# RWKV layers: loras on scaled weights, products beside the block solution, four recurrence lanes, fewer read-back transfers

## The chip, the core and the metric

The kernel runs on one core of one Trainium2 chip. Five engines work from queues of their own, each in the order of its program: TensorE (matrix products into PSUM), VectorE, ScalarE, GpSimd and SyncE, and 16 DMA engines move data for all of them. An engine that comes to an instruction whose input is not there waits, and all that is queued behind it on that engine waits too. The metric is the device time of one execution in microseconds; the time of before is the median of three runs.

## What is computed

The reference is a block of four layers, each with a feed-forward part, a mixer and a second feed-forward part, and a second block behind them, over 256 tokens of width 1024 in float32. The mixers of layers 0 and 3 are RWKV-7, and the change touches only these:

```python
dx = token_shift(h) - h
xr, xw, xk, xv, xa, xg = [h + dx * mu[j] for j in range(6)]
r, k, v = xr @ w_rkv[0], xk @ w_rkv[1], xv @ w_rkv[2]
w = -jax.nn.softplus(-(w0 + jnp.tanh(xw @ w1) @ w2)) - 0.5
decay = jnp.exp(-jnp.exp(w.astype(f32)))
a = jax.nn.sigmoid(a0 + (xa @ a1) @ a2)
v = v + (v_first - v) * jax.nn.sigmoid(v0 + (xv @ v1) @ v2)   # layer 3 only
g = jax.nn.sigmoid(xg @ g1) @ g2
# 16 heads of 64: a state of 64 x 64 per head, updated token by token from
# decay, k, v, a and the normalised direction of k * k_k, and read by r;
# then a norm over the head, a bonus (r * k * r_k) summed times v, times g, @ w_o
```

## The kernel before

Tensors lie transposed, channels on the partitions: eight tiles of 128 channels by 256 tokens, so tile k holds heads 2k and 2k+1. A projection is done in split precision: weights and inputs are cut into a high and a low part, and each product is three matmuls (`mm3`, L379 to L381). A weight tile `raw` (128x1024) is loaded on SyncE's queue, its high part `wh` made by ScalarE (L292), the low part `wl` by VectorE (L371); three `raw` buffers are in turn. One tile of a projection takes eight such triples, 24 matmuls.

The recurrence is done in chunks of 64 tokens, four per tile. Within a chunk the token-by-token dependence is a triangular system of 64 unknowns per head and chunk, cut into two halves of 32. The program of one RWKV layer, `rwkv(l, j)`, in its order:

- *keys*: `mixed(2)` makes h, dx and the split key input (L670 to L675); `project(1)` follows tile by tile. `plain` (L684) makes the mixed inputs xw and xa of the decay and rate loras, `lora` (L697) and `lora_up` (L707) their two products each. `directions` (L748 to L753) norms the keys. Some steps of the first four value products (`values`, tile name `pval`) are beside them.
- *decay and factors*: a running sum of the log decays (L761, a scan), its exponentials (L763 to L772), and the scaled keys, directions and receptances of each pair of tiles (`factors`, L782 to L785, one of them on GpSimd). A product `pd` (L793) gives the triangular matrices, which ScalarE copies and stores to DRAM as dL (L798).
- *solution*: `solve` loads dL back as LT, one system per partition (L809, ScalarE's queue), and does forward substitution in 31 steps of two VectorE operations (L821, L822), each over all 128 systems. Results T and U are stored to DRAM (dTU, L826) and read back by head (L835 and L836, 24 loads of 32 partitions on ScalarE's queue). Beside it stand the receptance products (`project(0)`; `receive`, L876, multiplies them in), `grams` (L890 on TensorE, masked by VectorE in L891) and the gate's mixed input.
- *lanes*: `recur(k)` for each tile: bonus product `bo` (L922) of `rk` (L918), turning keys and values to token order (`tok` L930, `tokv` L938), `inverse` (px L904, pt L909: the half of the inverse that couples the two halves of 32), then four chunks, each with products `pc` for the right side (L951, L954), the solution (L959), the new state (L964) and the output (L973, L975). Three lanes work side by side, `LANES = ((0, 3, 6), (1, 4, 7), (2, 5))`, starting 0, 4 and 8 steps late; the remaining four values, the closing of each pair of tiles (head norm, bonus, gate product `pgt`) and the output projection `pjrwo` are woven into them.

`weave` calls a list of generators in turn, one step each; this and the builder's own scheduling set the order in which instructions stand on each engine. Names: GM are the masked grams, SR the receptances and scaled directions, AK the scaled keys, UV the values and solved rows by token, `st` the state.

## Time and profile before

| | |
|---|---|
| median of the runs | 3050.86 us (3048.76 to 3070.9) |
| the profiled execution | 3068.02 us, span 3066.2 us |
| mean granted clock of TensorE | 0.963 |
| TensorE / VectorE / ScalarE / GpSimd busy | 2889.8 / 2245.3 / 1587.3 / 64.3 us |
| RWKV of layer 0 | 225 to 538.9 us of the span |
| RWKV of layer 3 | 2045 to 2359.6 us |

A window row gives, for one stretch, the busy time of each engine with the number of instructions, then the granted clock as a share of full speed and the share of the DMA engines. The clock is at one of two levels, 1.2 or 2.4 GHz, so that 0.50 means the lower one throughout. A busy share says nothing of who waits for whom; for that the profile has waits, each with the instruction that ended it.

### The profile page before, as it was taken

Reading aid. Unit: us, or ns where it says so; the run is one execution under the profiler, and the core shown is the slowest. Engines: PE = TensorE matmul, PEld = TensorE weight load, DVE = VectorE, ACT = ScalarE, POOL = GpSimd, SP = SyncE. Lnnn points to the kernel's source line nnn. Section 1 sums busy time; section 2 is a strip of 40 time slices with the busy share of each in tenths; the row PEclk is TensorE's granted clock in tenths of the full one; section 3 lists DMA queues with packets and bytes.
Section 4 is the critical chain, followed back from the end, with each engine's and each line's share of the span. In section 5 each row is a group of like instructions: output and inputs, shape, how many; then the busy total and the mean of one; then the engine's idle time right before and its main releaser. Section 6 shows DMA issues by size and latency. Waiting matters only on the chain. (4 is left out here: it accounts for less than half of the span.)

```text
span 3066.2 us, 57996 instructions
## 1 busy us (share of the span) xinstructions
PE 2889.8 (94%) x23318; PEld 2736.4 (89%) x23318; DVE 2245.3 (73%) x3912; ACT 1587.3 (52%) x2746; POOL 64.3 (2%) x71
## 2 busy tenths in 40 slices
PE   7999699999998999999999999989599999999998
PEld 6987577999997989999988999988488999889898
DVE  8888724888787888888887888787635767566754
ACT  5547134545446765455466545446145546644543
POOL 0000000000000100000000000000000000000000
PEclk9999779999999999999999999999699999999899
DMA  8983312787884547887844887864303665544464
GB/s 320 333 308 106 103 33 75 258 298 265 295 278 158 165 142 223 293 289 278 297 157 143 289 310 256 295 204 126 91 23 121 199 183 179 180 144 130 152 185 132
DMA packets 196031, 614.47 MB, mean 200 GB/s; under 512 B 41137, under 2 KB 45105, under 8 KB 195762
## 3 DMA queue, kind: packets, MB, share of 16 engines
q1 hardware_dynamic: 169234, 596.54, 59.1%
q10 hardware_dynamic: 24544, 7.87, 1.1%
q0 software_dynamic: 1984, 6.36, 0.6%
q8 instruction: 183, 3.00, 0.4%
q14 instruction: 86, 0.70, 0.1%
HBM read 604.36 MB, written 6.32 MB: 199 GB/s over the span
## 5 line engine op out<-in xcount | busy, mean ns | idle before, releaser
L292 ACT ACTIVATE wh<-raw 128x1024 fp32r<-128x1024 f32 (+3 forms) x859 | 887.0, 1036 | 948.5 <-DMA raw<-in_wi 239.9
L371 DVE TENSOR_TENSOR wl<-raw,wh 128x1024 fp32r<-128x1024 f32 (+3 forms) x859 | 1030.5, 1202 | 388.7 <-ACT wh L292 381.6
L380 PE MATMUL pjwi<-xl,wh 128*128 128x256 f32 x2568 | 722.3, 283 | 3.9 <-DVE xl L504 3.5
L381 PE MATMUL pjwi<-xh,wl 128*128 128x256 f32 x2568 | 718.1, 281 | 0.2 <-DVE wl L371 0.2
L379 PE MATMUL pjwi<-xh,wh 128*128 128x256 f32 x2568 | 714.6, 282 | 3.2 <-ACT xh L292 1.8
L380 PEld LDWEIGHTS pjwi<-xl,wh 128*128 128x128 f32 x2568 | 483.7, 189 | 6.4 <-DVE xl L504 6.2
L381 PEld LDWEIGHTS pjwi<-xh,wl 128*128 128x128 f32 x2568 | 484.7, 189 | 0.4 <-DVE wl L371 0.4
L379 PEld LDWEIGHTS pjwi<-xh,wh 128*128 128x128 f32 x2568 | 480.0, 189 | 3.8 <-ACT xh L292 2.0
L380 PE MATMUL pdwo<-gl,wh 128*128 128x256 f32 x1408 | 395.6, 281 | 0.0
L381 PE MATMUL pdwo<-gh,wl 128*128 128x256 f32 x1408 | 395.5, 281 | 0.0
L379 PE MATMUL pdwo<-gh,wh 128*128 128x256 f32 x1408 | 394.7, 280 | 0.0
L420 DVE SCALAR_TENSOR_TENSOR aring<-aring,cbc 128x1024 f32<-128x1024 f32 x286 | 343.4, 1219 | 3.2 <-DMA aring<-in_adaw 3.0
L379 PEld LDWEIGHTS pdwo<-gh,wh 128*128 128x128 f32 x1408 | 265.4, 188 | 0.0
L380 PEld LDWEIGHTS pdwo<-gl,wh 128*128 128x128 f32 x1408 | 265.1, 188 | 0.0
L381 PEld LDWEIGHTS pdwo<-gh,wl 128*128 128x128 f32 x1408 | 264.8, 188 | 0.0
L381 PE MATMUL pjw2i<-xh,wl 128*128 128x256 f32 x416 | 118.8, 286 | 0.0
L379 PE MATMUL pjw2i<-xh,wh 128*128 128x256 f32 x416 | 118.2, 284 | 0.0
L380 PE MATMUL pjw2i<-xl,wh 128*128 128x256 f32 x416 | 117.7, 283 | 0.0
L379 PE MATMUL pjmbi<-xh,wh 128*128 128x256 f32 x352 | 101.1, 291 | 6.2 <-DVE cv L1076 3.7
L380 PE MATMUL pjmbi<-xl,wh 128*128 128x256 f32 x352 | 101.7, 290 | 0.6 <-DVE xl L504 0.6
L381 PE MATMUL pjmbi<-xh,wl 128*128 128x256 f32 x352 | 99.7, 284 | 0.3 <-DVE wl L371 0.3
L292 ACT ACTIVATE gh<-g 128x256 fp32r<-128x256 f32 x198 | 80.1, 405 | 33.5 <-DVE g L596 20.0
(516 smaller groups left out, 5922.2 us busy)
## 6 DMA issues: line engine op xcount, KB each, us to landing
raw<-in_wi SPq DMA_DIRECT2D x352, 512.0 KB, 4.6
aring<-in_adaw SPq DMA_DIRECT2D x286, 512.0 KB, 5.3
raw<-in_wo SPq DMA_DIRECT2D x128, 512.0 KB, 4.8
raw<-in_w2i SPq DMA_DIRECT2D x56, 512.0 KB, 3.8
raw<-in_wo SPq DMA_DIRECT2D x64, 384.0 KB, 4.5
raw<-in_rkv SPq DMA_DIRECT2D x48, 512.0 KB, 4.4
raw<-in_mbi SPq DMA_DIRECT2D x48, 512.0 KB, 3.6
raw<-in_fg SPq DMA_DIRECT2D x22, 512.0 KB, 4.3
```

The source lines that it names most:

```text
L292: ins = self.nc.scalar.activation(out, in_, func, **k)
L371: self.last = self.nc.vector.tensor_tensor(lo, src, hi.bitcast(F32), SUB)
L379: mm(out, a, xh[:parts, k, :], start=start, stop=False)
L380: mm(out, a, xl[:parts, k, :], start=False, stop=False)
L381: mm(out, b, xh[:parts, k, :], start=False, stop=stop)
L420: ins = nc.vector.scalar_tensor_tensor(raw, raw, 1.0, self.cbc, MUL, MUL, accum_out=m[:, b % 24:b % 24 + 1])
```

## The change

1. The first products of the decay and rate loras (w1 and a1) are one matrix `wa1` of 128 columns, and are computed as h times W plus dx times (mu times W): VectorE scales the weights (L694 of the new kernel) in place of mixing the inputs. The gate's input is mixed into dx itself. The second products keep their number.
2. `directions`, `decay` and `factors` follow each other for each pair, two pairs at a time, with 44 of 72 steps of all eight value products beside them.
3. `solve` loads LT in two halves, as soon as each half of the factors is there, in eight loads that alternate between ScalarE's and GpSimd's queues. The stores of T and U go one to each queue. The read-back is six loads of 32 partitions by 32 systems, three on each queue. Beside the steps stand the other values, the first four receptances, the gate's loras, and grams, `bo`, `tok` and `tokv` of the first four tiles (`tokens`).
4. Four lanes work on tiles n and n+4, starting one step apart. The inverse of a tile is a generator of its own ahead of its chunks. Receptances, grams, tokens and inverses of the last four tiles are woven into the lanes. The state is kept by halves of heads: each new state is two operations over 64x64 into a tile that was zeroed once, in place of one of 128x128 by a mask and an addition. The bonus is kept in the values' own tile.

```diff
-LANES = ((0, 3, 6), (1, 4, 7), (2, 5))
-STAGGER = (0, 4, 8)
-FILL = 1
-VALUES = 4
+STAGGER = (0, 1, 2, 3)
+SOLVED = 4
...
+        def lora_wa(dst):
...
+            for k0 in (0, 4):
+                ws.append(self.sp.tile([P, 512], F32, tag="b2", name="wmu", bufs=3))
+                f4 = lambda ap: ap.rearrange("p (k i n) -> p k i n", k=4, i=2)
+                V.tensor_tensor(f4(ws[-1]), f4(w[:, P * k0:P * k0 + 512]), bc(mu[:, k0:k0 + 4, :, None], [P, 4, 2, 64]), MUL)
+            for k in range(KT):
+                mm(ps[:, :T], w[:, k * P:k * P + P], h[:, k, :], start=k == 0, stop=False)
+                mm(ps[:, :T], ws[k // 4][:, k % 4 * P:k % 4 * P + P], dx[:, k, :], start=False, stop=k == KT - 1)
+                yield
...
         def solve():
-            while len(factored) < KT:
-                yield
             LT = self.b8("LT", F32, (P, 2, 1024))
...
-            for c in range(4):
-                self.bounce.dma_start(L[32 * c:32 * c + 32].rearrange("p (i j) -> p i j", j=32),
+            queues = self.bounce, nc.gpsimd
+            for half in range(2):
+                while len(factored) < 4 * half + 4:
+                    yield
+                for c in range(4):
+                    o = 64 * half + 16 * c
+                    queues[c % 2].dma_start(l3[o:o + 16], dL[8 * half:8 * half + 8].rearrange("q (b x) -> (q b) x", b=2)[:, :32 * T].rearrange("g (i x) -> g i x", x=T)[:, :, 64 * c:64 * c + 32])
...
             for u, src in enumerate((Tm, L)):
-                self.bounce.dma_start(dTU[u].rearrange("c g i q -> (c g i) q"), src)
...
-                for c in range(4):
-                    block = lambda u, i: dTU[u, c, o // 8:o // 8 + 8, i].rearrange("g (r t) -> r g t", t=32)
-                    for i in range(2):
-                        self.bounce.dma_start(U[0][o + 32 * i:o + 32 * i + 32, c, :, 32 * i:32 * i + 32], block(1, i))
-                    self.bounce.dma_start(U[1][o:o + 32, c], block(0, 0))
+                queues[u].dma_start(dTU[u].rearrange("h x i q -> (h x i) q"), src)
+
+            for half in range(2):
+                o = 64 * half
+                block = lambda u, i: dTU[u, half, :, i].rearrange("x (r t) -> r x t", t=32)
+                for n, (dst, src) in enumerate(((U[1][o:o + 32], block(0, 0)), (U[0][o + 32:o + 64, :, 32:], block(1, 1)), (U[0][o:o + 32, :, :32], block(1, 0)))):
+                    queues[(n + half) % 2].dma_start(dst, src)
+            solved.append(True)
...
-        weave([keys, chain(plain(1, xw), plain(4, xa), mixed(3, xv)), chain(directions(0), directions(2))])
-        weave([directions(4), directions(6)])
+        weave([keys, chain(*loras), mixed(3, xv)])
...
-        weave([project(0, xr, receive), chain(factors(0), factors(4)), chain(factors(2), factors(6)), solve(), chain(*(grams(k) for k in range(KT))), plain(5, xg)])
+        values_ = chain(*(values(k) for k in range(KT)))
+        ahead = lambda k0: chain(directions(k0), decay(k0), factors(k0))
+        weave([chain(ahead(0), ahead(4)), chain(repeat(None, 2), ahead(2), ahead(6)), islice(values_, 44), chain(repeat(None, 4), mixed(0, xr))])
...
-                    new = q1("st"), None
-                    V.scalar_tensor_tensor(new[0], p4, SC[:, k, c:c + 1], blk, MUL, MUL)
-                    if c:
-                        V.tensor_tensor(new[0], new[0], st[1], ADD)
+                    new = sts[c % 2]
+                    for h_, r in enumerate(H2):
+                        if c:
+                            V.scalar_tensor_tensor(hc(new[r], h_), hc(p4[r], h_), SC[r, k, c:c + 1], hc(old[r], h_), MUL, ADD)
+                        else:
+                            V.tensor_scalar(hc(new[r], h_), hc(p4[r], h_), SC[r, k, c:c + 1], None, MUL)
...
+        rs = project(0, xr, receive, [[i] for i in range(4)])
+        weave([solve(), values_, rs, chain(repeat(None, SOLVED), gates()), chain(*(chain(grams(k), tokens(k)) for k in range(4)))])
...
-        lanes = [chain(repeat(None, n), *(recur(k) for k in lane)) for n, lane in zip(STAGGER, LANES)]
-        weave(lanes + [chain(repeat(None, FILL), *(values(k) for k in range(VALUES, KT)))] + [closing(k) for k in range(0, KT, 2)] + [splits()])
+        lanes = [chain(repeat(None, s), inverse(n), recur(n, sts(n)), recur(n + 4, sts(n))) for n, s in enumerate(STAGGER)]
+        rs = project(0, xr, receive, [[i] for i in range(4, KT)], "ax")
+        weave(lanes + [rs, chain(*(chain(grams(k), tokens(k), inverse(k)) for k in range(4, KT)))] + [closing(k) for k in range(0, KT, 2)] + [splits()])
```

Where instructions come to stand, in the built programs, is shown at three places. First VectorE's row in layer 0 from the end of the factors to the first step of the solution (fs and LT), before:

```order
L813 MEMSET LT 128x1024
L876 TENSOR_TENSOR SR<-SR,pjrkv 128x256
L814 MEMSET LT 128x32
L371 TENSOR_TENSOR wl<-raw,wh 128x1024
L735 TENSOR_SCALAR rest<-par 128x8
L876 TENSOR_TENSOR SR<-SR,pjrkv 128x256
L891 TENSOR_TENSOR GM<-pg,crw 128x512 x14
L876 TENSOR_TENSOR SR<-SR,pjrkv 128x256
L371 TENSOR_TENSOR wl<-raw,wh 32x1024
L821 TENSOR_TENSOR fs<-LT 128x31
```

The same place in the changed kernel, from the last factor (L800):

```order
L800 TENSOR_TENSOR AK<-AK,IP 128x8x64
L752 TENSOR_SCALAR rest<-par 128x8
L906 TENSOR_TENSOR GM<-pg,crw 128x512
L368 TENSOR_TENSOR wl<-raw,wh 128x1024
L906 TENSOR_TENSOR GM<-pg,crw 128x512
L891 TENSOR_TENSOR SR<-SR,pjrkv 128x256
L368 TENSOR_TENSOR wl<-raw,wh 128x1024
L844 TENSOR_TENSOR fs<-LT 128x31
```

Of 14 gram products two are left in front of the first step, and of three receptances one; the others stand among the steps or behind them, the last four tiles' in the lanes.

Second, TensorE's row around the first bonus product `bo`, which waits for VectorE's `rk`; before (ahead of these rows eight triples of `pval`):

```order
L922 MATMUL bo<-rk,cbase 128x256
L930 MATMUL tok<-cbase,AK 128x128 x4
L938 MATMUL tokv<-crw,Vv 64x128 x4
L904 MATMUL px<-T_3844,GM 32x32 x8
L954 MATMUL pc<-UV,GM 64x64
L909 MATMUL pt<-U,X_3967 32x32 x8
```

In the changed kernel (ahead of these rows, since the last `pd`: eight loras, eight gram matmuls and 72 of the split products):

```order
L941 MATMUL bo<-rk,cbase 128x256
L945 MATMUL tok<-cbase,AK 128x128 x4
L712 MATMUL lora<-dx,raw 32x256 x4
L953 MATMUL tokv<-crw,Vv 64x128 x4
L712 MATMUL lora<-dx,raw 32x256 x4
L905 MATMUL pg<-SR,AK 128x128 x8
L941 MATMUL bo<-rk,cbase 128x256
L945 MATMUL tok<-cbase,AK 128x128 x4
L953 MATMUL tokv<-crw,Vv 64x128 x4
L979 MATMUL pc<-UV,GM 64x64 x2
L905 MATMUL pg<-SR,AK 128x128 x8
L941 MATMUL bo<-rk,cbase 128x256
```

Grams and tokens of the first four tiles now stand between the first `bo` and the first inverse. The `rk` of the first `bo` stands on VectorE behind step 22 of 31 (before: in the last step), that of the second in front of the last step, the other two behind the solution.

Third, ScalarE's row around the read-back, before (T and U in all 24 loads, cut here):

```order
L826 DMA dTU_2768<-LT 128x1024 x2
L292 ACTIVATE AK<-tok 128x512
L836 DMA T_3844<-dTU_2768 32x8x32 x2
L835 DMA U<-dTU_2768 32x8x32 x6
L836 DMA T_3844<-dTU_2768 32x8x32
L835 DMA U<-dTU_2768 32x8x32 x2
```

In the changed kernel:

```order
L850 DMA dTU_2764<-LT 128x1024
L289 ACTIVATE AK<-tok 128x512
L289 ACTIVATE UV<-tokv 64x512
L289 ACTIVATE r_3985<-pc 64x128
L856 DMA T_3425<-dTU_2764 32x32x32
L856 DMA U<-dTU_2764 32x32x32 x2
L289 ACTIVATE AK<-tok 128x512
```

Three loads are left on ScalarE, behind three copies that wait for TensorE. The other store and the other three loads stand on GpSimd, behind two zeroings and, of the values, the last store to vf (in layer 3 loads of vf).

## Rows read from the trace of the kernel before

**Rows 1.** Windows, layer 0, one stage each; (x) counts instructions, PEclk the mean clock
```profile
225.00:275.80 50.80, 44.63 (x279) 36.83 (x278) 44.76 (x107) 33.08 (x70) 0.69 (x1) 0.91 0.24 77
275.80:322.70 46.90, 40.95 (x348) 37.40 (x346) 36.96 (x53) 29.85 (x56) 8.46 (x7) 0.93 0.46 148
322.70:344.70 22.00, 21.94 (x189) 20.29 (x191) 13.52 (x25) 1.65 (x2) 0.00 (x0) 0.77 0.23 43
344.70:375.70 31.00, 10.05 (x60) 6.98 (x59) 28.47 (x73) 7.03 (x10) 2.48 (x3) 0.71 0.37 126
375.70:390.20 14.50, 4.18 (x29) 3.15 (x27) 0.82 (x2) 1.27 (x3) 1.80 (x1) 0.62 0.49 118
390.20:538.90 148.70, 146.07 (x1200) 118.05 (x1201) 51.73 (x116) 65.87 (x165) 3.43 (x4) 0.88 0.17 54
```

**Rows 2.** The same windows for the last four stages of layer 3
```profile
2149.30:2170.70 21.40, 21.40 (x179) 19.72 (x175) 12.86 (x23) 1.65 (x2) 0.00 (x0) 0.76 0.23 44
2170.70:2200.90 30.20, 9.05 (x58) 6.22 (x56) 27.52 (x73) 6.77 (x9) 1.89 (x2) 0.71 0.40 123
2200.90:2216.50 15.60, 5.18 (x31) 3.88 (x31) 2.27 (x4) 1.32 (x3) 2.88 (x3) 0.61 0.53 133
2216.50:2359.60 143.10, 141.03 (x1203) 114.98 (x1204) 55.76 (x125) 66.45 (x165) 2.90 (x3) 0.91 0.18 57
```

**Rows 3.** The window in which the lanes of layer 0 begin
```profile
390.00:411.50 21.50, 21.26 (x129) 16.64 (x129) 2.23 (x6) 5.73 (x17) 0.00 (x0) 0.50 0.02 4
```

**Rows 4.** Tile dL, layer 0: ns min/median/max, start times, landing
```profile
L798 ACTq DMA_DIRECT2D dL<-tm x8: 582/618/672, 304.6 to 325.5; - x8
L809 ACTq DMA_DIRECT2D LT<-dL x4: 353/584/709, 328.2 to 329.9; - x4
...
DMA to landing us min/median/max: 2.4/3.6/4.5
```

**Rows 5.** Lines, VectorE, 344.6 to 376: busy us, mean ns, idle before
```profile
L822 DVE TENSOR_TENSOR LT<-LT,fs 128x31 f32<-128x31 f32 (+15 forms) x31 | 10.6, 342 | 0.9
...
L371 DVE TENSOR_TENSOR wl<-raw,wh 128x1024 fp32r<-128x1024 f32 (+1 forms) x5 | 6.1, 1218 | 0.2 <-ACT wh L292 0.2
```

**Rows 6.** A window of projection matmuls alone, columns as in rows 1
```profile
253.00:260.00 7.00, 7.00 (x61) 7.00 (x60) 7.00 (x17) 4.73 (x13) 0.00 (x0) 1.00 0.01 2
```

**Rows 7.** Lines by form, layer 0, VectorE: mixes and directions
```profile
L371 DVE TENSOR_TENSOR ml<-mx,mh 128x256 fp32r<-128x256 f32 x24 | 9.4, 421 | 1.7 <-ACT mh L292 0.7
...
L753 DVE SCALAR_TENSOR_TENSOR KK<-AK,par,sq 128x256 f32<-128x256 f32 x8 | 3.4, 480 | 0.0
...
L749 DVE TENSOR_SCALAR sq<-ss 128x512 f32<-128x512 f32 x4 | 2.7, 684 | 0.0
```

**Rows 8.** Tile dac (Mamba layer): GpSimd's loads, and the landing of them
```profile
L1170 POOL DMA_DIRECT2D M<-dac x8: 537/566/595, 961.4 to 1069.1; - x8
...
DMA to landing us min/median/max: 1.7/4.4/10.0
```

**Rows 9.** Waits of ScalarE, layer 0: us in total, times, longest
```profile
ACT UV L292 <- DMA T<-dTU: 12.2, 1, 12.2
```

**Rows 10.** DMA, ScalarE's queue q10: 376.5 to 391.5, then 327.5 to 334
```profile
q10 hardware_dynamic: 6713, 1.41, 43.2%
...
q10 hardware_dynamic: 4179, 0.53, 53.3%
```

**Rows 11.** Lines by form, TensorE: 340 to 354 (pg), then 411.5 to 450
```profile
L890 PE MATMUL pg<-SR,AK 64*128 64x128 f32 x32 | 3.4, 284 | 0.0
...
L938 PE MATMUL tokv<-crw,Vv 128*64 128x128 f32 x16 | 2.2, 279 | 0.0
...
L922 PE MATMUL bo<-rk,cbase 128*128 128x256 f32 x4 | 1.3, 404 | 0.0
L930 PE MATMUL tok<-cbase,AK 128*128 128x128 f32 x8 | 1.2, 273 | 0.0
```

More of the change, by code (lines that the diff above doesn't have):

```diff
@@ L32 @@
 FIRST = (0, 0, 1, 0, 1, 1)
-VFIRST = 12
 DECAY = math.exp(-0.5)
@@ L701, in lora, with lora_up, project @@
             yield
[L703 removed]
+        def lora_up(name, idx, m, t, ups):
             w = self.get(name, idx, 0, 1024, m, whole=True)
             for k in range(KT):
[L706 to L709 removed]
+                for r, bias, dst in ups:
+                    ps = self.ax("up")
+                    mm(ps[:, :T], w[r, k * P:k * P + P], t[0][r], start=True, stop=True)
+                    act(dst(k), c8(ps[:, :T]), AF.Sigmoid, bias=self.p(bias, k))
+                if k % 2 or len(ups) > 1:
                     yield
[L712 to L714 removed]
+        def project(n, x, done, groups=(range(4), *([i] for i in range(4, KT))), tag="mm"):
+            for i0 in groups:
+                outs = yield from self.proj_steps([("rkv", (j, n, i)) for i in i0], x, tag=tag)
                 for i, ps in zip(i0, outs):
                     done(i, ps[:, :T])
[L718 to L719 removed]
+        xk, xr, xv, xg = [], [], [], [dx]
+        lwa, lv, lg1, lg2 = ([] for _ in range(4))
         finish(mixed(2, xk, True))
@@ L934, in recur @@
                 nc.gpsimd.memset(UVs[half][top], 0.0)
-            UV = UVs[half][:, k % 4]
             pv = self.ax("tokv")
@@ L938, in recur @@
                 mm(pv[bot, P * c:P * c + P], Vv[:, k, 64 * c:64 * c + 64], C["cen"], start=True, stop=True)
-            act(UV[bot], pv[bot], AF.Copy)
+            act(UVs[half][bot, k % 4], pv[bot], AF.Copy)
+            V.tensor_tensor(Vv[:, k], bo[:, :T], Vv[:, k], MUL)
             yield
-            yield from inverse(k)
+        def recur(k, sts):
+            while k not in ready:
+                yield
+            half, n = k // 4, 2 * (k % 4)
+            top = H2[half]
+            GM = GMs[k // 2][:, k % 2]
+            UV = UVs[half][:, k % 4]
+            both = AK[half][:, k % 4].rearrange("p c q t -> p (c q t)")
             pc = self.mm("pc")
@@ L950, in recur @@
                 if c:
-                    mm(p1, SR[:, 0, k, f], st[0], start=True, stop=False)
+                    mm(p1, SR[:, 0, k, f], st, start=True, stop=False)
                 for h_ in range(2):
@@ L974, in recur @@
                 if c:
-                    mm(py[:, f], st[0], SR[:, 1, k, f], start=False, stop=True)
+                    mm(py[:, f], st, SR[:, 1, k, f], start=False, stop=True)
                 st = new
@@ L998, in close @@
             for d, k in ks:
-                V.tensor_tensor(pair(y)[:, d], pair(y)[:, d], bons[k], ADD)
+                V.tensor_tensor(pair(y)[:, d], pair(y)[:, d], Vv[:, k], ADD)
             pg = self.ax("pgt")
@@ L1008, in close, with gates @@
             closed.add(k0)
-        bons, pys = {}, {}
-        finish(chain(*gate))
-        self.table(TABLE_NORM)
+        pys, lgs, wg = {}, [], []
+        def gates():
+            yield from gate_mix()
+            self.table(TABLE_SIGM)
+            yield from lora("g1a", (j,), xg, 128, AF.Sigmoid, lg1)
+            yield from lora("g1b", (j,), xg, 32, AF.Sigmoid, lg2)
+            for t, n in ((lg1[0], 128), (lg2[0], 32)):
+                lgs.append([self.sp.tile([P, 1, T], F32R, tag="lo", name="lgs", bufs=5) for _ in range(2)])
+                self.split(t[:n], lgs[-1][0][:n, 0], lgs[-1][1][:n, 0])
+            self.table(TABLE_NORM)
+            yield
+        rs = project(0, xr, receive, [[i] for i in range(4)])
+        weave([solve(), values_, rs, chain(repeat(None, SOLVED), gates()), chain(*(chain(grams(k), tokens(k)) for k in range(4)))])
+        ST = self.b8("ST", F32, (P, 8, P))
+        nc.gpsimd.memset(ST, 0.0)
         wg1, wg2 = self.get("g2a", (j,), 0, 1024, 128), self.get("g2b", (j,), 0, 1024, 32)
-        lgs = []
-        for t, n in ((lg1[0], 128), (lg2[0], 32)):
-            lgs.append([self.sp.tile([P, 1, T], F32R, tag="lo", name="lgs", bufs=5) for _ in range(2)])
-            self.split(t[:n], lgs[-1][0][:n, 0], lgs[-1][1][:n, 0])
         def closing(k0):
```

97 lines of the change are left out of this document (45 added, 52 removed).

## The prediction

> **What bounds the kernel now.** The page shows TensorE busy almost everywhere and no line of its chain stands out, so the average tells little; the change touches only the two RWKV layers, 314 us each of the 3066. I therefore cut each layer into stages at the instructions that hand one stage to the next and read the busy time of the engines in them [rows 1, 2]. In layer 0 TensorE is busy 44.6 of 50.8 us up to the first scan, 41.0 of 46.9 up to the last factor, 21.9 of 22.0 until the block solution starts, 10.1 of 31.0 while VectorE does it, 4.2 of 14.5 while its result goes to DRAM and back, and 146 of 148.7 in the lanes. Layer 3 repeats this. So there are two kinds of loss: a hole of some 31 us (21 in the solution, 10 in the read-back), and time at half clock: a stretch with a mean granted clock of 0.88 spends 0.24 of itself at the lower of the two levels and loses half of that, 17.8 us in the lanes of layer 0 and 0.09 x 143.1 = 12.9 us in those of layer 3. The lanes begin with 21.5 us at 0.50 [rows 3]: TensorE had been idle or broken for 36 us before.
>
> The path that sets the lanes' start is: last factor, its product stored to dL, LT loaded, 31 steps, store of T and U, read-back. The store and the load take about 3.6 us each from issue to landing [rows 4]. The last LT load was issued 329.9 us into the span, some 7 us after the last factor, so LT was there at 333.4; but the first step ran at 344.7, because VectorE, in order, had 14 GM products and three SR products in front of it that wait for TensorE. That is 11 us of wait with the data there. The 31 steps are 2 x 10.6 us and a copy, and five wl and a few others lie between them [rows 5].
>
> **The change, term by term, for layer 0.**
>
> *Up to the first scan.* The four value products go behind it (12 of their steps stood ahead, 2.4 values x 24 matmuls x 7.00/61 us = 6.6 us [rows 6]). Lora and up matmuls are as many as before, 16 and 16. The loras on scaled weights start with h itself, in the first 20 us, where most of TensorE's 6.2 idle us of this stage lie, and two VectorE products replace 16 mixes of KK's length. So the first scan comes 7 us earlier (0 to 10). From there to the last factor VectorE gets more: it was busy 37.0 of 46.9 us [rows 1]; it gains the directions (4 x 0.68 and 8 x 0.48 us), eight ml (8 x 0.42) and four more wl (4 x 1.22), and loses three SR products (1.2): 37.0 + 6.5 + 3.4 + 4.9 - 1.2 = 50.6 us [rows 5, 7]. It is now the engine that sets this stage; TensorE has little but values beside it. With 2 us of waits the stage takes 52.5 us, 5.6 more, and the last factor comes 7 - 5.6, about 2 us earlier. From below: no waits and all 10 us, -7; from above: the same share of waits as now, 50.6 x 46.9/37.0 = 64 us, +10.
>
> *From the last factor to the first step.* The GM and SR products in front of the solution fall from 17 to five or so, and half of LT is loaded earlier. What is left is the latency: product and issue 2.3 us, 3.6, and 3.6, about 10 us in place of 22.0: -12. Four of the loads now go over GpSimd. No row has a load of many short rows on that queue; the nearest, M, took 4.4 us in the median and 10.0 at worst from issue to landing [rows 8]. I take the 3.6 of ScalarE's queue, as the loads of a half are small; the other end is +13 (two in sequence at 10.0).
>
> *The 31 steps.* Between them now stand six wl, two rk, and one each of SR, Vv, GM and a split: about 10 us in place of 8.8: +1.5 (0 to +4).
>
> *Read-back.* ScalarE waited 12.2 us in its own 24 issues before it could copy tokv [rows 9]; three issues each on two queues replace them. But the transfers themselves were 43.2% of 16 engines over 15 us, 6.5 us at full rate with the end of the store among them, and LT's four loads show what a burst does, 53.3% of 6.5 us for 4096 rows, 3.5 us [rows 10]: 6144 rows need 5.2 us. The inverses of the first four pairs need only the first half of it. So 2.7 us of store, 0.5 of issue, 5.2 and about 1.5 of latency: 10 in place of 14.5, -4.5 (-7 to 0 by ScalarE's rows). The Trainium skill ("DMA: Bandwidth & Descriptors", "Issuing engines are not separate DMA queues") says that issuing on several engines saves only the time on the sequencer, which is usually small beside the transfer. By that rule this term and the earlier LT load would be near nothing, some 9 us less gain over both layers. Here the row disagrees with "usually": 24 issues were the longer part, since the engines stood at 0.43. The number of issues is what counts, the second queue little.
>
> *The lanes.* Of the 148.7 us, 2.6 are idle and 17.8 lost to the clock, so 128.3 us is work at full speed. Moved: three token steps go out ahead of the lanes (bo 1.3/2, tok about the same, tokv 2.2/2: 2.35 us each, -7.1), grams of four pairs come in (1.7 us each, +6.8), and four receptance products stand where three values stood (+2.8) [rows 11]: +2.5. The inverses stay. The split state update (two 64x64 operations for one or two of 128x128) is on VectorE, busy 51.7 of 148.7: nothing, as long as four lanes give TensorE something to do. The clock: TensorE's row now runs receptances, values and grams, then bo of the first pair, which waits for rk behind step 22; from there tokens, loras and grams follow with short gaps until the inverses. That is 15 to 20 us of work ahead of the lanes, where before the clock came back 21.5 us after such a start. I take 4 us of clock loss and 2.6 idle: 128.3 + 2.5 + 6.6 = 137.4, -11. From below: the clock as now, 151, +2.5; from above: none lost, -15.
>
> Sum for layer 0: -2 - 12 + 1.5 - 4.5 - 11 = -28 us.
>
> **Layer 3** has the same program with a value residual: three VectorE operations and one load for each value. Four values more stand ahead of the end of the solution, 4 x 3 x 0.42 = 5 us, half of it in the steps. Last factor 0; first step -11 (of 21.4); steps +2.5; read-back -5 (of 15.6); lanes 128.1 + 2.5 + 2.1 + 4 = 136.7 for 143.1, -6.4. Sum -20 us. On GpSimd's queue some of these loads stand ahead of the store of U, waiting for their tiles; I cost that at nothing, since they are issued steps earlier, and at one landing, 3 us, if not.
>
> Together -48 us of the profiled 3068.02: 3020. That execution stood 17 us above the median of the runs shown, so I predict 3003 us.
>
> **Rivals.**
> *A. VectorE's factor stage waits as now.* For it: 10 of the 46.9 us there are waits, and directions, scans and factors are now one chain through three engines. Against it: two chains run side by side. Last factor +10 instead of -2 in layer 0, likewise in layer 3: 24 us of the gain gone, 3027.
> *B. The hole only moves.* For it: bo of the first pair still stands behind step 22, and TensorE's work between the last pd and it (8 grams matmuls 1.7, 72 of the projections 8.3, eight loras of about 0.5) is 14 us at full clock against 35 us. If the clock then falls again and the lanes begin as now, the lanes' term is +2.5 in both layers: 22 us less, 3025.
> *C. All holes filled.* Last factor -7 in both layers, no clock lost in the lanes, loads at the lower ends: a further 12 us each, 2979.
> *D. GpSimd's loads are slow (the other side).* Two LT loads and a store with up to two of three read-backs follow each other on that queue, and the lanes' start hangs on them. At 10.0 us each, the worst landing of [rows 8], the first step comes 13 us later than forecast and the read-back takes 30 in place of 10: 33 us per layer, and the clock falls as now, 10 more per layer: 3003 + 86 = 3089, slower than before. It decides from about 6 us each on, where the forecast's gain is used up. Against it: the median of [rows 8] is 4.4 for four times the bytes of such a load. The Trainium skill has the rule behind it ("DMA: Bandwidth & Descriptors", "SWDGE vs HWDGE vs iDMA"): descriptors of GpSimd's transfers are written by its software, those of ScalarE's by hardware. No row shows how this grows with short rows.
>
> **How the numbers follow.** Forecast 0.45 (its own range 2985 to 3020), A 0.16, B 0.16, C 0.13, D or a weaker form of it 0.10. A change under 1% can't be told from none here; 1% is 30.5 us, so faster means below 3020. That holds for the forecast but a twentieth, for C, and for a fifth or so of A and B: 0.43 + 0.13 + 0.06 = 0.62. The full D gives slower, about half of its share with a little for two mishaps together: 0.06. The rest, 0.32, is same. The range leaves out the lower half of C and D: 2973 to 3045.
>
> **What would show it.** Right: the first step of the solution within 12 us of the last factor; 31 steps in 32 to 35 us; the first px within 10 us of the last step; the first 20 us of the lanes at a clock above 0.75; lanes of about 137 us in both layers. Wrong: GpSimd's loads landing above 6 us (D), px waiting for them; the last factor later than 100 us after the layer's start (225) in layer 0, with VectorE below 80% busy ahead of it (A); bo's wait for VectorE still near 20 us and lanes beginning at 0.50 (B). If TensorE in the lanes shows waits for ScalarE or VectorE of more than 5 us, the split state update or the late bonus of the second four pairs is the cause, and no term above has it.

## The result, and the profile after

The changed kernel takes 3094.17 us, the median of four runs (3078.62 to 3109.58), against 3058.8 us of four runs of the kernel before. The ratio is 1.0121, with a 95% interval of 1.0081 to 1.0161: slower by 1.2%. The forecast was 3003 us in 2973 to 3045, and slower by over 1% had a chance of 0.06. The profiled execution took 3078.62 us (span 3076.8), the best of the four, so its trace shows less of the loss than the median has. From here on, medians are of all runs of a kernel, and ratios leave out the runs that lay over 1.5% above its fastest (seven in all).

Windows of layer 0 in the changed kernel, cut at first mix, first scan, last factor, first step, end of the steps, first px, end. In [rows 1] the last stage begins at 390.2, where TensorE went on behind the loads; the first px of that kernel had run in pieces from 379.2 on, waiting for them.

```profile
228.10:256.20 28.10, 26.93 (x174) 24.45 (x174) 24.81 (x59) 18.17 (x48) 0.00 (x0) 0.90 0.24 61
256.20:307.60 51.40, 47.27 (x405) 41.41 (x404) 44.25 (x75) 40.25 (x82) 9.93 (x12) 0.97 0.50 147
307.60:323.50 15.90, 12.70 (x102) 11.04 (x103) 4.32 (x8) 4.70 (x7) 4.64 (x6) 0.97 0.58 141
323.50:356.30 32.80, 15.29 (x88) 11.43 (x86) 30.11 (x75) 9.12 (x12) 2.33 (x2) 0.70 0.34 103
356.30:366.20 9.90, 9.29 (x79) 7.43 (x77) 5.70 (x11) 3.25 (x6) 3.90 (x5) 1.00 0.73 203
366.20:552.40 186.20, 182.31 (x1279) 148.72 (x1279) 62.38 (x138) 65.78 (x161) 1.80 (x1) 0.73 0.16 49
```

Layer 3 in the same way, from the first scan (first mix at 2048.9):

```profile
2077.50:2137.50 60.00, 51.61 (x421) 43.01 (x420) 47.32 (x86) 41.57 (x87) 9.53 (x10) 0.97 0.40 117
2137.50:2152.30 14.80, 13.22 (x114) 11.76 (x114) 6.61 (x11) 4.38 (x5) 4.27 (x5) 1.00 0.71 147
2152.30:2190.70 38.40, 18.94 (x101) 14.22 (x102) 33.37 (x85) 10.07 (x13) 2.92 (x3) 0.72 0.37 113
2190.70:2201.30 10.60, 10.40 (x75) 8.31 (x73) 4.81 (x11) 2.98 (x5) 3.81 (x5) 0.90 0.69 157
2201.30:2367.40 166.10, 163.18 (x1262) 133.91 (x1262) 59.83 (x132) 65.27 (x160) 1.80 (x1) 0.80 0.16 51
```

The reader is to see that the lanes begin sooner, and that the last rows give this back: TensorE is busy 182 of 186 us there, as it was 146 of 148.7 in [rows 1], but its mean granted clock fell from 0.88 to 0.73, in layer 3 from 0.91 to 0.80. Measured from the first mix (before: 226.5 and 2045.1) and between like instructions, the terms of the sum came out so, in us. The steps end with the copy behind them (375.7 and 2201.9 before, 357.0 and 2190.7 now) and the layer with its last write (541.6 and 2360.1 before), which moves some borders of the windows by up to 2.7 us:

| term | layer 0 forecast | measured | layer 3 forecast | measured |
|---|---|---|---|---|
| last factor | -2 | -16.6 | 0 | -15.0 |
| last factor to first step | -12 | -6.2 | -11 | -7.2 |
| 31 steps | +1.5 | +2.5 | +2.5 | +7.2 |
| steps to lanes | -4.5 | -5.3 | -5 | -4.0 |
| lanes to the layer's end | -11 | +34.8 | -6.4 | +22.5 |
| sum | -28 | +9.2 | -20 | +3.5 |

The lanes begin 26 and 19 us sooner than before, more than forecast, and give back 35 and 22. The parts between and behind the two layers took 2 us less together. The other runs agree: the mean clock was 0.942 to 0.955 over the four, and 0.961 to 0.970 over 20 runs of the kernel before; multiplied with the times, 54 us more are lost to the clock, for 35 us more time.

Where the clock went is shown by windows of the lanes of layer 0:

```profile
366.20:373.80 7.60, 7.60 (x139) 6.51 (x138) 0.90 (x3) 3.96 (x11) 0.00 (x0) 0.99 0.01 2
373.80:421.20 47.40, 47.40 (x244) 37.78 (x243) 8.96 (x25) 10.21 (x33) 0.00 (x0) 0.50 0.04 12
421.20:424.90 3.70, 3.70 (x43) 2.96 (x41) 0.57 (x2) 0.92 (x3) 0.00 (x0) 0.96 0.00 0
424.90:445.20 20.30, 20.30 (x110) 15.74 (x110) 3.87 (x8) 6.70 (x17) 1.80 (x1) 0.50 0.09 27
445.20:458.90 13.70, 13.70 (x119) 10.72 (x118) 6.88 (x16) 6.05 (x14) 0.00 (x0) 1.00 0.01 1
458.90:478.00 19.10, 19.10 (x89) 15.49 (x87) 4.55 (x9) 5.16 (x13) 0.00 (x0) 0.50 0.08 28
```

and of layer 3:

```profile
2201.30:2206.80 5.50, 5.50 (x99) 4.63 (x99) 0.42 (x1) 3.01 (x8) 0.00 (x0) 0.98 0.02 3
2206.80:2256.30 49.50, 49.50 (x276) 39.67 (x275) 9.02 (x25) 10.78 (x34) 0.00 (x0) 0.50 0.03 11
2256.30:2316.00 59.70, 58.95 (x532) 46.75 (x531) 24.11 (x54) 27.86 (x70) 1.80 (x1) 0.99 0.10 31
```

The lanes start at full clock in both layers. It falls 7.6 and 5.5 us later, without any idle time of TensorE, and stays at the lower level for 47 and 50 us in which TensorE is never idle either. What it did before and after the first fall of layer 0 is told by the groups by line, first of 366.2 to 373.8, then of 373.8 to 418, then of 418 to the rise at 421.2 (some of the groups of each):

```profile
L922 PE MATMUL px<-T,GM 32*32 32x32 f32 x64 | 2.7, 192 | 0.0
L927 PE MATMUL pt<-U,X 32*32 32x32 f32 x48 | 2.1, 192 | 0.0
...
L979 PE MATMUL pc<-UV,GM 128*64 128x64 f32 x42 | 7.1, 316 | 0.0
L989 PE MATMUL pc<-UV,AK 128*128 128x128 f32 x18 | 7.0, 492 | 0.0
L984 PE MATMUL pc<-r,U 64*64 64x64 f32 x36 | 6.4, 326 | 0.0
...
L953 PE MATMUL tokv<-crw,Vv 128*64 128x128 f32 x8 | 2.0, 428 | 0.0
```

The fall stands behind the first inverses of four tiles in a bunch, 112 matmuls of 32x32 in 7.6 us; the chunks' products fill most of the half-speed stretch, and 24 matmuls of the receptances (128x128 against 256 columns) among them did not bring the clock back; the rise comes right behind the next tokv, of tile 4. In layer 3 it is the same sequence. The next three falls of layer 0 each followed a single inverse, and the rise at 445.2 two products of 512 columns of a head norm. The kernel before had its inverses one at a time and the tokens of seven tiles spread over the lanes; once its clock was up, it lost it for 10 us (449.7 to 459.9) and for 3 in layer 0, and for 3 in layer 3.

### The profile page after: what moved, and what is told of

Same layout as the page of the kernel before. It is cut to its first block, busy times and chain, and to the rows that moved or that the text cites. A ratio compares the mean times of both kernels' runs of the same rounds, so it can differ in the third digit from the quotient of the medians.

```text
span 3076.8 us, 57978 instructions
## 1 busy us (share of the span) xinstructions
PE 2919.7 (95%) x23318; PEld 2759.0 (90%) x23318; DVE 2229.1 (72%) x3884; ACT 1591.4 (52%) x2762; POOL 77.8 (3%) x89
```

## The experiments

All ratios are to runs of the kernel before on the same chip (medians 3051 to 3059 us). Differences in us between two changed forms are taken between their ratios, 1% being 30.6 us; a ratio's interval is 0.4 to 1% wide, so they hold to some 10 to 20 us. The windows show one execution of each kernel, up to 17 us off its median. They run from the first px to the end of the layer; for the kernel before these are

```profile
379.20:541.60 162.40, 150.28 (x1238) 121.77 (x1238) 54.43 (x120) 67.79 (x169) 4.90 (x5) 0.86 0.20 58
2205.40:2360.10 154.70, 143.04 (x1223) 116.55 (x1224) 56.68 (x127) 67.18 (x166) 5.36 (x6) 0.89 0.20 59
```

**More work in the lanes.** To tell a loss by the clock from a loss by waits, matmuls were added.

```diff
+                for _ in range(2):
+                    mm(pc[H2[1 - half], P:2 * P], blk[:, :64], C["cen"], start=True, stop=True)
                 for h_ in range(2):
                     mm(hc(p3, h_), U[0][top, 8 * c + n + h_], hc(r1[top], h_), start=True, stop=True)
```

> The changed kernel with 64 more matmuls per RWKV layer, two in each chunk of each tile, of the form of tokv (128 rows by 64 columns of a constant against 128 columns), into a part of the chunk's PSUM bank that nobody reads. Nothing is left out. At full clock they cost 64 x 0.28 us = 18 us per layer. Theory 1 (the lanes lose their gain to TensorE's clock, 0.73 in layer 0 and 0.80 in layer 3, and what raises the clock are matmuls that use the whole array, as before the two rises at 421 and 445 us): the clock in the lanes goes above 0.9, the lanes of layer 0 take about 132 + 18 + 10 = 160 us instead of 186, those of layer 3 about 155 instead of 166, and the kernel is 20 to 40 us faster than the changed one although it does more. Theory 2 (four lanes in step are slow because TensorE, in order, waits for their copies, and the low clock only follows from that): the extra work fills waits and costs nothing, or comes on top: 0 to 36 us slower than the changed kernel, clock within 0.05 of before.

Measured: 3052.2 us, ratio to before 0.9991 (0.9955 to 1.0027), 40 us faster than the changed kernel with more to do. The lanes of layer 0, the first 61 us of those of layer 3, and all of the latter:

```profile
367.00:528.50 161.50, 157.02 (x1402) 128.66 (x1402) 62.14 (x137) 64.58 (x160) 1.80 (x1) 0.99 0.18 56
...
2170.60:2176.90 6.30, 6.30 (x126) 5.51 (x126) 0.43 (x1) 3.22 (x9) 0.00 (x0) 0.98 0.01 3
2176.90:2232.00 55.10, 55.10 (x281) 43.28 (x280) 9.03 (x25) 10.70 (x34) 0.00 (x0) 0.50 0.03 10
2170.60:2353.50 182.90, 179.32 (x1386) 145.85 (x1386) 59.82 (x132) 64.95 (x160) 1.80 (x1) 0.83 0.15 46
```

Layer 0 did as theory 1 said: no fall in the first 137 us, 161.5 us in all. Layer 3 did not: the clock fell behind the first inverses as before, just ahead of the first added product, and the 20 added ones of the next 23 us did not bring it back. The loss is the clock's; in this layer it begins behind the bunch of inverses.

**The same time of another form.** A control for the last run: the added products on 64 rows by 64 columns.

```diff
-                    mm(pc[H2[1 - half], P:2 * P], blk[:, :64], C["cen"], start=True, stop=True)
+                    mm(pc[H2[1 - half], P:2 * P], blk[H2[1 - half], :64], C["cen"][H2[1 - half]], start=True, stop=True)
```

> Control for the run with 64 added matmuls: the changed kernel with as many at the same places and of the same length, but with 64 rows by 64 columns of weights (the form of the chunks' own products) instead of 128 by 64. Nothing is left out. Theory 1 (the form of TensorE's work decides whether the clock stays): lanes' clock as in the changed kernel, within 0.08 of 0.73 and 0.80, and 15 to 50 us slower than it, since the added work is paid at half clock. Theory 2 (any added work fills waits and so raises the clock): as the run with tokv's form, clock 0.83 to 0.99 in the lanes, 30 us or more faster than the changed kernel.

Measured: 3072.25 us, 1.0035 (1.0013 to 1.0056).

```profile
365.90:543.60 177.70, 172.79 (x1402) 140.30 (x1402) 62.25 (x137) 64.55 (x160) 1.80 (x1) 0.82 0.16 50
2186.10:2369.30 183.20, 179.26 (x1386) 144.82 (x1386) 59.89 (x132) 64.82 (x160) 1.80 (x1) 0.77 0.15 46
```

This lies between the theories, so the control settles less than it should. It is 13 us slower than the run with tokv's form, at the edge of what the intervals tell apart, and the clock fell behind the first inverses in both layers and not in one; but it is 26 us faster than the changed kernel, which theory 1 had not expected. The form seems to matter, and so does something that any added work does; what, is open.

**The bunch itself.** Eight added matmuls behind px of each of the first four inverses, nowhere else.

```diff
             act(x[b], px[b, :256], AF.Copy)
+            if k < 4:
+                for u in range(8):
+                    mm(px[H2[1 - k // 4], 256:384], blk[:, :64], C["cen"], start=True, stop=True)
             yield
```

> The changed kernel with 32 added matmuls of tokv's form per layer, eight behind the px of each of the first four inverses and nowhere else, into unread PSUM. Nothing is left out. They cost 32 x 0.28 = 9 us per layer at full clock. In the run with 64 added matmuls spread over the chunks the clock of layer 0's lanes was 0.99, but in layer 3 it fell right behind the bunch of first inverses (103 matmuls of 32x32 in the 6 us from 2171) and stayed at 0.50 for 55 us. Theory 1a (that bunch is where the clock is lost; the lanes then do not win it back for long): no fall in the first 30 us of the lanes, their clock above 0.85 in both layers, 25 us or more faster than the changed kernel (3094) in spite of 18 us of added work. Theory 1b (the bunch is only the first place where it falls, the lanes lose it anyway): the fall comes some 10 to 20 us later, lanes' clock below 0.80, no more than 10 us faster.

Measured: 3040.53 us, 0.9963 (0.9927 to 0.9999): 48 us faster than the changed kernel, with half the added work of the first run.

```profile
366.20:520.60 154.40, 150.16 (x1334) 125.22 (x1334) 62.08 (x137) 64.86 (x160) 1.80 (x1) 0.96 0.19 58
2171.00:2342.10 171.10, 166.43 (x1325) 138.10 (x1325) 59.91 (x132) 65.72 (x160) 1.80 (x1) 0.84 0.16 50
```

The fall behind the first inverses is gone in both layers. In layer 3 another came 46 us into the lanes, behind px of tile 4, and held until the next tokens, and one more after that: theory 1a for the first and largest loss, 1b for the rest.

**Lanes further apart, and three lanes.** First four lanes with a wider start:

```diff
-STAGGER = (0, 1, 2, 3)
+STAGGER = (0, 2, 4, 6)
```

> The changed kernel with its four lanes started 0, 2, 4 and 6 steps late in place of 0, 1, 2 and 3. Theory 1a (it is the bunch of the four first inverses, 64 matmuls of 32x32 within 8 us, that lets the clock fall at 374 us, after which it is slow to return): the first fall comes later or not at all, the clock of the first 50 us of the lanes is above 0.75 (0.56 in the changed kernel), 15 us or more gained in all. Theory 1b (the clock falls for what the lanes lack over their whole length, work on the whole array): the stagger moves the falls but not their share: lanes' clock within 0.06 of 0.73 and 0.80, time within 15 us. Theory 2 (waits of lanes in step): a few us gained per layer with the clock as it was.

Measured: 3051.22 us, 0.996 (0.9925 to 0.9994), 49 us faster than the changed kernel.

```profile
363.90:531.30 167.40, 164.31 (x1278) 134.46 (x1278) 62.55 (x138) 65.30 (x160) 1.80 (x1) 0.84 0.18 55
2185.70:2353.60 167.90, 165.74 (x1262) 135.76 (x1262) 60.22 (x132) 65.26 (x160) 1.80 (x1) 0.81 0.16 50
```

The time did as theory 1a said, the clock of these windows less so. Two steps are still a bunch: in layer 0 the first fall came at about 375 us, 11 us into the lanes, and lasted some 27 us in place of 47; in layer 3 it came 5 us in and lasted 37 in place of 50. The first 50 us of the lanes ran at 0.73 and 0.62, under the 0.75 expected. Then the lanes of before in the changed kernel:

```diff
-STAGGER = (0, 1, 2, 3)
+LANES = ((0, 3, 6), (1, 4, 7), (2, 5))
+STAGGER = (0, 4, 8)
...
-        lanes = [chain(repeat(None, s), inverse(n), recur(n, sts(n)), recur(n + 4, sts(n))) for n, s in enumerate(STAGGER)]
+        lanes = [chain(repeat(None, s), *(chain(inverse(k), recur(k, sts(n))) for k in LANES[n])) for n, s in enumerate(STAGGER)]
...
```

> The changed kernel with the three lanes of before (tiles 0, 3, 6 and 1, 4, 7 and 2, 5, started 0, 4 and 8 steps late, each tile's inverse right ahead of its chunks); everything ahead of the lanes and the receptances, grams and tokens beside them as changed. Theory 1a: inverses spread over the lanes as before, so the clock holds: lanes' clock back to about 0.88, 25 us or more gained. Theory 1b: the beside-work is still that of the changed kernel, so the clock stays under 0.82 and the gain under 15 us. Theory 2: lanes as fast as before in full, some 30 us per layer gained, whatever the clock.

Measured: 3027.83 us, 0.9896 (0.9845 to 0.9947), 69 us faster than the changed kernel and 1.0% faster than the one before.

```profile
366.70:513.20 146.50, 142.90 (x1278) 118.28 (x1278) 62.43 (x138) 65.16 (x160) 1.80 (x1) 0.98 0.19 62
2164.10:2312.60 148.50, 145.43 (x1262) 120.30 (x1262) 59.99 (x132) 65.07 (x160) 1.80 (x1) 0.93 0.17 57
```

Theory 1a: the same beside-work, the same count of matmuls, and no fall in the first 120 us of layer 0's lanes. In layer 3 one came 84 us in and lasted 13.7 us, with no 32x32 product in the 4 us ahead of it: bunches of inverses are not the only place. This form also puts the inverses of the last four tiles back into the lanes. And these three lanes in step:

```diff
-STAGGER = (0, 4, 8)
+STAGGER = (0, 1, 2)
```

> The kernel with three lanes in front-changed form (3028 us), its lanes started 0, 1 and 2 steps late in place of 0, 4 and 8. Theory 1a (lanes in step bunch their inverses and that costs the clock): three inverses in a bunch instead of four; the clock falls early in the lanes of at least one layer, lanes' clock under 0.88 (0.98 and 0.93 with the wide start), 10 to 30 us slower than 3028. Theory 3 (the number of lanes decides: with four a round of the weave holds one receptance triple and one gram or token step for four chunk steps, with three for three): clock as with the wide start, within 0.05, time within 8 us of 3028.

Measured: 3053.16 us, 0.9988 (0.9956 to 1.002), 28 us slower than with the wide start.

```profile
364.70:516.80 152.10, 148.04 (x1278) 122.04 (x1278) 62.11 (x138) 65.15 (x160) 1.80 (x1) 0.93 0.19 60
2169.60:2345.30 175.70, 173.05 (x1261) 141.74 (x1261) 59.63 (x132) 65.13 (x160) 1.80 (x1) 0.76 0.15 48
```

Layer 3 lost the clock 5 us into the lanes, for 72 us; layer 0, with the same three inverses in a bunch, kept it for the first 50 us and more. So of the 69 us between four lanes in step and three apart, some 28 belong to the start and 41 to the fourth lane and the inverses that moved with it.

**Tokens back in the lanes.** Bonus, tok and tokv of the first four tiles ahead of each lane's inverse instead of beside the solution:

```diff
-        weave([solve(), values_, rs, chain(repeat(None, SOLVED), gates()), chain(*(chain(grams(k), tokens(k)) for k in range(4)))])
+        weave([solve(), values_, rs, chain(repeat(None, SOLVED), gates()), chain(*(grams(k) for k in range(4)))])
...
-        lanes = [chain(repeat(None, s), inverse(n), recur(n, sts(n)), recur(n + 4, sts(n))) for n, s in enumerate(STAGGER)]
+        lanes = [chain(repeat(None, s), tokens(n), inverse(n), recur(n, sts(n)), recur(n + 4, sts(n))) for n, s in enumerate(STAGGER)]
```

> The changed kernel with the bonus, tok and tokv products of the first four tiles put back into the lanes, each lane's ahead of its first inverse; they no longer stand beside the solution. Theory 1a: products on the whole array now stand between the inverses, so the clock is not lost there: lanes' clock above 0.85, 20 us or more faster than the changed kernel although 8 us of TensorE's work per layer move from the hole of the solution into the lanes. Theory 1b or 3: the fall comes a little later, lanes' clock within 0.06 of 0.73 and 0.80, time within 12 us of the changed kernel.

Measured: 3070.95 us, 1.0025 (0.999 to 1.006).

```profile
361.40:558.80 197.40, 192.28 (x1294) 157.20 (x1294) 64.19 (x142) 68.27 (x166) 1.80 (x1) 0.69 0.15 46
2205.00:2358.90 153.90, 149.31 (x1278) 123.62 (x1278) 61.49 (x136) 68.47 (x166) 1.80 (x1) 0.91 0.18 55
```

Inconclusive: layer 3 did as theory 1a said; in layer 0 the clock fell 3.5 us into the lanes, behind the first inverse and a wait of TensorE of 1.4 us, and stayed at the lower level for 92 us. Why the layers differ is open.

**The transfers alone**, in the kernel before: `solve` with the loads and stores of the change's diff, and the layout that goes with them.

```diff
-        dTU = self.dp.tile([2, 4, 2 * KT, 2, 1024], F32, name=f"dTU_{l}")
+        dTU = self.dp.tile([2, 2, 32, 2, 1024], F32, name=f"dTU_{l}")
...
-                    mm(hc(p3, h_), U[0][top, c, n + h_], hc(r1[top], h_), start=True, stop=True)
+                    mm(hc(p3, h_), U[0][top, 8 * c + n + h_], hc(r1[top], h_), start=True, stop=True)
```

> The kernel of before with the changed transfers of the solution alone: LT in eight loads by halves, T and U stored on two queues, six read-back loads, the layout of U that goes with them. All else as before. By the prediction's terms: read-back 4.5 us shorter in each layer, ScalarE no longer held for 12 us; LT may come earlier but the products in front of the first step still hold VectorE, so nothing there. 5 to 12 us faster than before in all, if the clock at the start of the lanes is as it was (back after about 21 us). If GpSimd's loads were slow (rival D): 5 us or more slower.

Measured: 3027.2 us, 0.9907 (0.9872 to 0.9943): 32 us faster by the medians, 28 by the ratio, some three times what was expected. The windows are last factor to first step, end of the steps to first px, and the lanes, then the lanes of layer 3:

```profile
320.40:338.10 17.70, 16.99 (x194) 16.20 (x195) 14.04 (x24) 2.71 (x3) 4.45 (x6) 1.00 0.40 83
...
368.40:372.70 4.30, 2.72 (x14) 2.02 (x13) 0.77 (x2) 0.60 (x1) 2.14 (x3) 0.70 0.86 259
372.70:516.30 143.60, 139.62 (x1239) 113.99 (x1240) 54.47 (x121) 68.31 (x169) 6.09 (x7) 0.95 0.22 66
2171.40:2309.10 137.70, 133.64 (x1223) 109.59 (x1224) 56.44 (x127) 67.38 (x166) 6.63 (x8) 0.98 0.21 65
```

From first px to the end, layer 0 lost 12.1 us idle and 0.14 x 162.4 = 22.7 to the clock before, and loses 4.0 and 7.2 now. Layer 3 gains 17.0 us in the same window. These two executions lie 52 us apart, 20 more than the medians, so the windows show too much of it; but by the clocks of all runs, in the mean 0.965 before and 0.973 now, 25 of the 34 us between the mean times are the clock's. The stall of the read-back had kept TensorE in pieces for 14 us. That this delayed the return of the clock is the likely reading, and not shown: with the same transfers and the loras (the last run below) the clock was slow to return again.

**One queue.** The same transfers, all from ScalarE:

```diff
-            queues = self.bounce, nc.gpsimd
+            queues = self.bounce, self.bounce
```

> The kernel of before with the changed transfers (3027 us), but all of them issued on ScalarE's queue, as many and as large: eight loads of LT, two stores, six loads back. The prediction held that the number of issues is what counts and the second queue little. If so: within 6 us of 3027. If the second queue is what freed ScalarE and TensorE: at least half of the 32 us go, 3043 or more. The 16 issues cost ScalarE about 16 x 0.46 = 7 us per layer in place of 4, partly where it waits anyway.

Measured: 3050.34 us, 0.9984 (0.9959 to 1.0009).

```profile
323.30:352.90 29.60, 25.45 (x220) 21.57 (x220) 16.12 (x28) 5.70 (x7) 1.89 (x2) 0.94 0.36 85
381.40:385.40 4.00, 2.65 (x13) 1.95 (x12) 0.74 (x2) 0.60 (x1) 1.02 (x1) 0.50 0.79 254
```

By the ratios 24 of the 28 us went, more than the half that was to speak for the second queue, but not where that queue would show: from the steps' end to px it took 4.0 us, against 4.3 on two queues. What grew is the way to the first step, 29.6 us for 17.7, because in this build four gram products came to stand behind the gate's loras on VectorE, in front of the first step, and waited 7.6 us for them; layer 3 has the same wait. The transfers agree with the rule of the Trainium skill ("DMA: Bandwidth & Descriptors", "Issuing engines are not separate DMA queues") that more issuing engines save only sequencer time; whether the later first step comes with one queue in any order was not tried.

**The loras alone**, in the kernel before:

```diff
...
-        weave([keys, chain(plain(1, xw), plain(4, xa), mixed(3, xv)), chain(directions(0), directions(2))])
+        weave([keys, mixed(3, xv), chain(directions(0), directions(2))])
...
-        loras = [lora("w1", (j,), xw, 64, AF.Tanh, lw), lora("a1", (j,), xa, 64, AF.Copy, la),
-                 lora_up("w2", (j,), 64, lw, f"w0{j}", lambda k: c8(SG[:, k])), lora_up("a2", (j,), 64, la, f"a0{j}", Aa)]
+        loras = [lora_wa(lwa), lora_up("wa2", (j,), P, lwa, [(H2[0], f"w0{j}", lambda k: c8(SG[:, k])), (H2[1], f"a0{j}", Aa)])]
...
```

> The kernel of before with the loras on scaled weights alone (and dx's first column on ScalarE). VectorE loses 16 mixes and 8 small operations per layer and gains two products, 8 us less; TensorE's work is the same. By the prediction's step the first scan comes earlier by at most a few us, since the value steps ahead of it stay: 0 to 5 us per layer, 0 to 10 us faster in all. If instead this part carries the 15 us by which the changed kernel's last factor came earlier in layer 0 (307.6 against 322.7 us): 20 us or more faster.

Measured: 3050.35 us, 0.9979 (0.9956 to 1.0002). The last factor came 7.7 us sooner in layer 0; 6 us are left of it, within what can't be told from nothing.

**Receptances ahead.** Two of them beside the factors, so that bo's wait goes; three lanes.

```diff
-        weave([chain(ahead(0), ahead(4)), chain(repeat(None, 2), ahead(2), ahead(6)), islice(values_, 44), chain(repeat(None, 4), mixed(0, xr))])
+        rs = project(0, xr, receive, [[i] for i in range(4)])
+        weave([chain(ahead(0), ahead(4)), chain(repeat(None, 2), ahead(2), ahead(6)), islice(values_, 27), chain(repeat(None, 4), mixed(0, xr), islice(rs, 17))])
...
```

> The changed kernel with three lanes (3028 us), and the receptances of the first two tiles computed beside the factors in place of two value products, which move beside the solution. rk, and with it bo, tok and tokv, of the first tiles then stand on VectorE behind steps 2, 12 and 20 of the solution instead of 22 and the last: the wait of bo, 17.5 us in the changed kernel, falls under 8 us in each layer. If TensorE's hole in the solution costs what it is long: 10 to 20 us faster than 3028, so 3010 to 3018, faster than both kernels. If the work that fills it is only taken from the read-back, where it covered the transfers: within 6 us of 3028, with px waiting for the loads instead.

Measured: 3059.09 us, 0.9988 (0.9955 to 1.002): 28 us slower than three lanes without it, which neither forecast had. The solution, the way to px, and the lanes of layer 0:

```profile
322.10:363.60 41.50, 31.46 (x184) 24.37 (x185) 34.67 (x85) 13.25 (x20) 4.30 (x5) 0.83 0.39 122
363.60:370.20 6.60, 3.14 (x16) 2.30 (x15) 0.42 (x1) 1.19 (x2) 2.93 (x4) 0.76 0.87 218
370.20:549.30 179.10, 175.82 (x1269) 145.53 (x1270) 62.18 (x137) 64.22 (x159) 1.80 (x1) 0.74 0.17 52
```

bo's wait fell to 8.6 us in layer 0, near the 8 expected, and two costs came out: the steps took 41.5 us where three lanes without this took 33.6, and TensorE, busy 3.1 of the 6.6 us ahead of the lanes, began them at the lower clock. It was back after 7 us, but fell three times more, for 21, 27 and 31 us, and the lanes ran at 0.74 (0.88 in layer 3). The kernel with the hole in the middle of the solution is the faster one; why the later falls came without it is not shown.

**Two parts together** in the kernel before: the diffs of the transfers and of the loras.

> Two parts of the change together on the kernel of before: the transfers of the solution (3027 us alone) and the loras on scaled weights (3050 us alone, 0.2% faster than before); three lanes and all other work as before. If the parts add up: 3018 to 3025 us, faster than both kernels. If the earlier last factor is only waited away, as VectorE has the same gram products in front of the first step: within 4 us of 3027. A clock in the lanes above 0.93 in both layers is expected in either case, as with the transfers alone.

Measured: 3023.23 us, 0.9897 (0.9862 to 0.9933), faster than both kernels. It can't be told from the transfers alone (0.9907), nor from the changed kernel with three lanes apart (0.9896). The clock above 0.93 did not come: in the profiled execution (3034.86 us) the lanes ran at 0.89 and 0.91. The first px came 4.5 us behind the steps, as with the transfers alone, but the clock, which falls there in both kernels, stayed at the lower level for 24 us in both layers, and for 7 with the transfers alone.

## Why the prediction was wrong

*The lanes* are the step that failed, the sentence "I take 4 us of clock loss", which stands in both layers' sums. By the windows, 186.2 us at a mean of 0.73 lose 0.27 x 186.2 = 50 us, layer 3 0.20 x 166.1 = 33 us. What is left, 136 and 133 us, is what was forecast without the clock (133.4 and 132.7). The work was counted rightly; the clock was asked only whether TensorE would be busy ahead of the lanes, and it was: 9.3 of 9.9 us at 1.00. That it can fall inside the lanes with no idle time stood in the trace of before,

```profile
450.00:458.00 8.00, 8.00 (x35) 6.07 (x35) 1.57 (x4) 1.88 (x6) 0.00 (x0) 0.50 0.01 2
```

and I had counted this stretch among the losses without asking what it came from. "The inverses stay" was right in number and wrong in order: four of them now stand in a bunch, and with larger products between these the first fall was gone in both layers. Why the clock falls where it does later, and what brings it back, stays open. No rival had this; B let the clock fall ahead of the lanes, at the price of before.

*Last factor*: forecast -2, measured -16.6. I had all eight key products ahead of the first scan. In the built program 44 of the 64 triples and 5 of the 16 second lora products ran ahead of it, the others beside the factors, so it came 28.1 us after the first mix and not 42. VectorE was busy 44.3 us in the stage behind it, not 50.6. Rival A is refuted: waits were 7 of 51 us.

*First step*: -6.2 for -12. The loads were mis-sized at 3.6 us. The last store to dL landed in 2.4 us, but the loads of LT's second half were issued 1.4 to 3.5 us after that, GpSimd's behind a store to vf that waited 2.7 us for its value, and landed after 5.0 to 7.5 us, on both queues; VectorE waited 2.6 us for the last. The DMA engines were busy 0.58 of this stage, 0.23 before [rows 1], with weights among the rest (loads issued in this stage, KB each, median us from issue to landing):

```profile
raw<-in_rkv SPq DMA_DIRECT2D x2, 512.0 KB, 6.1
...
LT<-dL ACTq DMA_DIRECT2D x2, 64.0 KB, 6.2
LT<-dL POOLq DMA_DIRECT2D x2, 64.0 KB, 7.4
```

That the weights made the loads of LT slow is argued, not tried.

*31 steps*: +2.5 for +1.5, and +7.2 for +2.5 in layer 3; VectorE was busy 33.4 us there, 27.5 before [rows 2], so what stands between the steps was counted too low.

*Read-back*: -5.3 for -4.5, and the covering work was there. Tile dTU of layer 0:

```profile
L856 POOL DMA_DIRECT2D U<-dTU x2: 783/789/795, 361.0 to 361.8; - x2
...
DMA to landing us min/median/max: 3.4/4.1/4.8
```

GpSimd's loads of 1024 short rows issue in 0.8 us, all transfers here landed within 4.8, and TensorE did not wait for them. One sign of rival D was there, GpSimd's loads of LT landing above 6 us (7.2 and 7.5); but ScalarE's beside them took 5.0 and 7.4, so it does not speak for a slow queue, and D's price did not come. The price of this stall was mis-sized in the other direction, as the transfers alone show: some 30 us and not 9, most of it clock.

*The hole*: rival B's wait was there,

```profile
PE bo L941 <- DVE rk L939: 17.5, 1, 17.5
```

and cost little, since the work behind it brought the clock back before the lanes.

*State update*: TensorE was idle for 3.9 of the 186.2 us of the lanes, and three lanes with the split update ran as fast as before, so it costs nothing that shows.

## What to carry to other kernels

A busy TensorE is not a fast one: multiply each stretch by its granted clock before taking its time for work, and ask of each change which stretches of small products it lays end to end, not only where it leaves TensorE idle. When several chains of small products are started together, start them apart, so that larger products fall between their like parts. And measure the parts of a large change one by one: here the transfers alone gained as much as everything but the fourth lane, and four lanes in step lost twice that.

## What was not expected of the hardware

The clock stayed at the lower level for 47 to 55 us, and once for 72, in which TensorE was not idle for 0.1 us. The longest of these stretches began behind bunches of 32x32 products, though not every bunch lost the clock, and ended mostly with the next tile's bo, tok and tokv; 20 products of tokv's form spread over 23 us did not end one. The Trainium skill ("TensorE: Matmul & The Clock Gate", "Part 1: The HAM clock gate") has the clock follow how busy TensorE has been of late. These rows do not agree: it was busy 47.40 of 47.40 us at 0.50. 32 added products per layer made a kernel some 50 us faster. And one program differs by 30 us from run to run, 3078.62 us at a mean clock of 0.955 and 3109.58 at 0.942 in the changed kernel.
